# Low parts of streamed weights: a subtraction on VectorE, or an accumulating transfer

## Chip, core and metric

One Trainium2 chip, one core. The metric is the device time of one execution, in microseconds (us). The kernel before takes 723.99 us (median of 3 runs, 723.56 to 726.15).

## What is computed

One layer of an encoder on 512 tokens of width 1024, in float32. In short:

```python
z = rms_norm(x, g_mix) @ W_in                  # 1024 -> latents, rotary key, HGRN2 q, f, i, gate
a = latent_attention(z)                        # 4 heads, softmax over 512 tokens
r = hgrn2(z)                                   # 4 heads, gated recurrence, chunks of 64, two directions
x = x + concat(a, r) @ W_o
h = rms_norm(x, g_ffn)
x = x + (silu(h @ W_gate) * (h @ W_up)) @ W_down          # width 2816
x = x + sigmoid(rms_norm(x, g_ple) @ W_pg) * (p @ W_pp)
```

## The kernel before, in words

**Precision.** TensorE multiplies in float32r, which keeps fewer bits than float32. So each operand is held as two float32r tiles, hi (the value rounded) and lo (the value minus hi), and a product is three matmuls, hi·hi, lo·hi and hi·lo (`mm3`, lines 136 to 139). Features lie on partitions, the 512 tokens on columns.

**Weights.** All large matrices are read from HBM once, in 114 chunks of at most [128, 1024] float32 (512 KB). `weights` (lines 143 to 151) makes one: SP's queue loads it into a tile `raw`, ScalarE rounds it to `whi` (line 130, in `split`), and VectorE subtracts, `wlo = raw - whi` (line 131). `raw` has RAWB = 4 buffers, `whi` and `wlo` WB = 3 each, used in turn. A load waits until both readers of that `raw` buffer are done; a `whi` waits for the matmuls of the chunk three before.

**Stages.** First the latents: five chunks of `w_q`, each with a piece of x, then three of `w_kv` (lines 223 to 257). Then two streams of work are merged (line 921): the latency stream (attention, then the recurrence by head) and the dense stream, which projects with 16 chunks of `w_hf` and 4 of `w_i` and later with the output matrix (`w_oa`, `w_or`) and `w_pp`. The dense stream takes its chunks from `wnext` (lines 560 to 565), which asks for a chunk one ahead of its use (AHEAD = 2) and gives the subtraction of every second chunk of the first 13 to GpSimd, not VectorE (LO_POOL = 14). Last come the feed-forward part (44 chunks of `w_gate` and `w_up`, tiles `ff`; 24 of `w_d`, tiles `dn`) and the embeddings (8 chunks of `w_pg`). One chunk feeds 24 matmuls of 512 columns (21 for most of `w_d`).

**Who else works around it.** In the gates of HGRN2 (lines 606 to 643) ScalarE makes sigmoids and logarithms (lines 613, 631) and has to load a table before each kind; VectorE makes the elementwise steps (lines 616, 618, 627, 628) and GpSimd two products (lines 621, 634). GpSimd also makes the rotary turns (lines 304 to 307), the power -1/2 in every norm (line 164) and the decays (lines 681, 698, 699). VectorE evacuates most PSUM tiles.

**Order.** Each engine runs its instructions in one fixed order and waits on semaphores. The tile framework sets that order when the kernel is built, from a timeline of its own (line 1074), so it is made anew for every version.

Of the kernel before, what the change touches and what calls it, by code (L numbers as in the profile page):

```python
# [8 lines left out]
F32 = mybir.dt.float32  # L9
# [15 lines left out]
# shares of the two streams  # L25
L_TOTAL, D_TOTAL = 97, 135
AHEAD = 2
WB = 3
RAWB = 4
# [3 lines left out]
LO_POOL = 14  # L33
# [3 lines left out]
# columns of the packed per-partition vectors  # L37
V_MIX, V_FFN, V_PLE, V_QA, V_KVA, V_QN, V_KN, V_LB, V_HGO = 0, 8, 16, 24, 26, 28, 29, 30, 46
NV = 50
# columns of the packed rows (the same for every partition)  # L40
R_QN, R_KN = 0, 64
NR = 128
# columns of the constants that depend on shapes alone
# [11 lines left out]
class Slots:  # L55
    """Tiles of one size, handed out by hand: the one that has been free longest comes next."""
# [19 lines left out]
    def part(self, prefix, n):  # L76
        """Slots of their own from the free ones."""
        s = Slots(self.pool, 0, self.prefix)
        s.free.extend(self.free.popleft() for _ in range(n))
        s.count = 1000 * ord(prefix)  # L80
        return s
# [7 lines left out]
def merge(streams):  # L89
    """Runs generators side by side, by the shares of their totals that they have yielded. One that  # L90
    yields a condition waits until it holds."""
    live = [[g, total, 0.0, None] for g, total in streams]
    while live:
        ready = [s for s in live if s[3] is None or s[3]()]
        s = min(ready, key=lambda s: s[2] / s[1])
        s[3] = None
        try:
            y = next(s[0])
        except StopIteration:
            live.remove(s)  # L100
            continue
        if callable(y):
            s[3] = y
        else:
            s[2] += y


def v3(t, a, b=None):
    """A tile's 512 columns as (a, b)."""
    return t.rearrange("p (a b) -> p a b", a=a)  # L110
# [3 lines left out]
def layer_kernel(ctx: ExitStack, tc: tile.TileContext, io, out):  # L114
# [11 lines left out]
    # ---------------------------------------------------------------- helpers  # L126
    def split(hi, lo, src, scale=None, eng=dve):
        """src (times a scale per partition) = hi + lo, each exact in float32r."""
        if scale is None:
            act.activation(hi, src, AF.Copy)  # L130
            eng.tensor_tensor(lo, src, hi, ALU.subtract)  # L131
        else:
            act.activation(hi, src, AF.Copy, scale=scale)
            dve.scalar_tensor_tensor(lo, src, scale, hi, ALU.mult, ALU.subtract)
# [8 lines left out]
    def weights(src, cols, lo_eng=None):  # L143
        """A chunk of weights [128, cols]: its parts hi and lo."""
        nw[0] += 1
        raw = wpool.tile([P, 1024], F32, tag="raw", bufs=RAWB, name=f"raw{nw[0]}")
        hi = wpool.tile([P, 1024], F32R, tag="whi", name=f"whi{nw[0]}")
        lo = wpool.tile([P, 1024], F32R, tag="wlo", name=f"wlo{nw[0]}")
        sp.dma_start(raw[:, :cols], src)
        split(hi[:, :cols], lo[:, :cols], raw[:, :cols], eng=lo_eng or dve)  # L150
        return hi, lo
# [7 lines left out]
    def rsqrt_mean(o, ss, n):  # L159
        """o = (ss / n + eps) ** -0.5, for a few columns."""  # L160
        w = ss.shape[-1]
        v = small.tile([P, 8], F32, tag="rs_v", name="rs_v")
        dve.tensor_scalar(v[:, :w], ss, 1.0 / n, EPS, ALU.mult, ALU.add)  # L163
        pool.tensor_tensor(o, v[:, :w], mhalf[:, :w], ALU.pow)  # L164

    def token_rstd(sq, keep=None):
        """From sums of squares [128 of the features, tokens]: 1/rms by token, tokens on
        partitions [128, 4] and on columns, the same on every partition [128, 512]."""
# [6 lines left out]
        # the diagonal matrices of 1 / rms, summed over the partitions  # L175
# [13 lines left out]
    def squares(acc, src, first):  # L189
        """acc += src ** 2"""  # L190
# [8 lines left out]
    # ---------------------------------------------------------------- inputs  # L199
# [11 lines left out]
    # loads the activation engine's table while the first inputs are under way  # L211
    act.activation(small.tile([P, 1], F32, tag="first", name="first"), mhalf[:, :1], AF.Exp)

    # ---------------------------------------------------------------- input projection, latents
    # the query's latents, features on partitions
    hT = [(A.get(f"hh{k}", F32R), A.get(f"hl{k}", F32R)) for k in range(KT)]
    cq = [B.get(f"cq{m}") for m in range(2)]
    # the tensor engine's clock rises while it is busy
# [4 lines left out]
    for ks in ((0,), (1,), (2, 3), (4, 5), (6, 7)):  # L223
        w = weights(io["w_q"][:, ks[0] * 256 : (ks[-1] + 1) * 256], len(ks) * 256)
# [25 lines left out]
    # those of key and value and the rotary key, tokens on partitions  # L250
    ckv = [B.get(f"ckv{j}") for j in range(NT)]
    for c, ks in enumerate(((0, 1, 2), (3, 4, 5), (6, 7))):
        w = weights(io["w_kv"][:, ks[0] * 320 : (ks[-1] + 1) * 320], len(ks) * 320)
# [20 lines left out]
    # ---------------------------------------------------------------- rotary tables  # L274
# [17 lines left out]
    # cos(r) = sin(pi / 2 - |r|)  # L292
# [9 lines left out]
    def rope(eng, o, x, c, s, t1, t2):  # L302
        """o = x * [cos, cos] + [x2, x1] * [-sin, sin], all [128, a, 64]"""
# [5 lines left out]
    # ---------------------------------------------------------------- lower bounds of the gates  # L309
# [14 lines left out]
    # ================================================================ latent attention  # L324
# [4 lines left out]
    def attention():  # L329
        """Emits the attention in pieces; yields the tensor engine's time for each."""  # L330
        # 1 / rms of the latents, with the one of the input
        sc = cpool.tile([P, 2 * NT], F32, name="sc")  # by token: query, key and value
# [28 lines left out]
        # the shared rotary key, with its gains, turned  # L361
# [8 lines left out]
        def wsmall(name, cols):  # L370
            """A small matrix of two chunks, two halves each."""
# [11 lines left out]
        # keys and values; per head, tokens on partitions: [128, tile, 128]  # L383
# [3 lines left out]
        rt = [A.get(f"rk{j}") for j in range(NT)]  # rotary parts by tile: [128, (key, query) x head, 64]  # L387
# [67 lines left out]
        def features(tok, g):  # L455
            """[128 tokens, tile, 128] to [128 features, tokens], times gains: hi and lo."""
# [9 lines left out]
        def rotary(pr):  # L466
            """Of two heads: the key's parts (hi, hi) and (lo, lo), the query's (hi, lo)."""
# [78 lines left out]
    # ================================================================ HGRN2  # L546
    # 1 at every step but a chunk's first, for the sums along the chunks
# [7 lines left out]
    # chunks of weights for the dense stream, one ahead of its use  # L555
    wlist = deque()
    ahead = deque()
    nd = [0]

    def wnext():  # L560
        while wlist and len(ahead) < AHEAD:
            nd[0] += 1
            on_pool = nd[0] % 2 == 0 and nd[0] < LO_POOL
            ahead.append(weights(*wlist.popleft(), pool if on_pool else dve))
        return ahead.popleft()

    def w_in_tile(d):
        """One tile of 128 of the input projection's columns: [128 columns, tokens]"""
# [11 lines left out]
    def w_in_tokens(evacuate):  # L580
        """512 columns of the input projection, tokens on partitions, 256 at a time."""
# [16 lines left out]
    def gates(heads):  # L598
        """q, and for each direction k and the sums of log f along the chunks."""
# [10 lines left out]
        # one table of the activation engine after the other  # L610
# [13 lines left out]
        for (h, d), f in zs.items():  # L624
            # log f = log max(f, c) + log min(f / c, 1)
# [17 lines left out]
    def together(emit):  # L643
        """The first, whose operand comes last, and the others right behind it."""
        first = emit[0]()
        with tc.issue_after(first.ins):
            for e in emit[1:]:
                e()

    def output_gates():  # L650
        """Features on partitions, with the gains of the output norm."""
# [19 lines left out]
    def decays(h):  # L671
        """Of one head, both directions: queries and keys with the decays that go with them."""
        yield lambda: ("gates", h) in done
        for d in range(2):
# [7 lines left out]
            # exponentials of the sums: to the chunk's middle, from there to its end, to its end  # L682
# [17 lines left out]
            # the same for tiles of two chunks  # L700
# [16 lines left out]
    def within(h):  # L717
        """What reaches a step from its own tile of two chunks, as weights [128 s, tile, 128 t]."""
        pd = BL.get("pd")  # within chunks: [128 (chunk, s), direction, tile, 64 t]
        pd4 = pd.rearrange("p (d j t) -> p d j t", d=2, j=NT)  # L720
        px = BL.get("px")  # from a tile's earlier chunk to its later one
# [27 lines left out]
    def carried(h):  # L749
        """The states before the tiles, both directions."""  # L750
# [50 lines left out]
    def finish(h):  # L801
        """Norm, gate and layout of one head's outputs."""
# [27 lines left out]
    def w_o_half(half, src, banks):  # L830
        """x += (src as rows of features) @ half of the output projection's rows"""
# [92 lines left out]
    def residual(m, o, g, sqacc, hs):  # L924
        """x[m] += o; its squares and its parts hi and lo, with the next norm's gains."""
# [17 lines left out]
    # ---------------------------------------------------------------- feed-forward  # L943
# [41 lines left out]
    # ---------------------------------------------------------------- per-layer embeddings  # L985
    rs3, bc3 = token_rstd(sq3)
    for m in range(KT):
        w = weights(io["w_pg"][m], 1024)
        # the last one in two parts, since nothing is left to overlap with it
# [16 lines left out]
def _layout(inp):  # L1006
# [10 lines left out]
    kp = lambda w: w.reshape(-1, P, w.shape[1])  # [k, 128, columns]  # L1017

    def chunks(w, n):  # n rows of 128 to a chunk: [chunks, 128, n * columns]
# [3 lines left out]
    def tiles(w):  # [tiles of 128 columns, 128, rows / 128 * 128]  # L1023
# [22 lines left out]
    t = tiles(f("w_ple_proj")[0])  # [8, 128, 256]  # L1046
# [32 lines left out]
```

## Time and profile before

| | |
|---|---|
| runs | 723.99 us median, 723.56 to 726.15 |
| span of the profiled execution, first to last instruction | 721.8 us |
| time of the profiled execution as a run | not listed; the median stands 2.2 us over its span |
| TensorE matmul busy | 703.6 us, 97% |
| VectorE, ScalarE, GpSimd busy | 439.3, 309.2, 135.8 us |
| HBM read | 63.68 MB, 91 GB/s over the span |

The profile is of one execution. A busy matmul unit is modelled from pipelined instructions, so it says that work was in flight, not that every cycle was used. "PEclk" is the clock granted to TensorE as a share of its full one. "DMA share" is the busy share of the core's 16 DMA engines. An entry "A <- B" of the waits says that A's engine sat idle until B was done. The chain is the sequence of work that ended last, followed back from the end.

### The profile page before, as it was taken

To read this page: it belongs to the slowest core of one execution; us is meant where nothing else is said; L and a number is where in the kernel's file an instruction comes from. 1 tells how busy PE (TensorE), PEld (TensorE's weight loads), DVE (VectorE), ACT (ScalarE), POOL (GpSimd) and SP (SyncE) were. 2 spreads that over 40 slices of the span, in tenths; PEclk is the share of its full clock that TensorE was granted. 3 is DMA by queue.
4 is the path that set the end of the run, shared out by engine and by line. 5 is a ranking of instruction groups with operands and counts; after the bars stand their busy time and mean duration, and the time that the engine had idled before them with its cause. 6 is when DMAs were issued, how large, how long until landed. Compare 5 with 4: busy or idle time off the path is not lost.

```text
span 721.8 us, 9167 instructions
## 1 busy us (share of the span) xinstructions
PE 703.6 (97%) x3516; PEld 588.5 (82%) x3516; DVE 439.3 (61%) x733; ACT 309.2 (43%) x573; POOL 135.8 (19%) x126
## 2 busy tenths in 40 slices
PE   8999997998999999999999999999999999999997
PEld 6888885897878888788888888888888888888886
DVE  8954469988999984386545334435433444456573
ACT  5566785576554635355233222223222223244341
POOL 7983577010543511001000000000000000000000
PEclk9999999999999999999999999999999999999999
DMA  8432112111034221033232322232233232233211
GB/s 282 167 114 93 59 36 81 59 30 60 15 103 156 60 78 59 30 118 116 96 109 87 104 101 87 91 114 77 79 108 117 90 108 87 78 105 116 89 59 58
DMA packets 22075, 66.36 MB, mean 92 GB/s; under 512 B 2704, under 2 KB 3984, under 8 KB 22032
## 3 DMA queue, kind: packets, MB, share of 16 engines
q1 hardware_dynamic: 22032, 65.79, 28.0%
q8 instruction: 27, 0.44, 0.2%
q14 instruction: 16, 0.13, 0.1%
HBM read 63.68 MB, written 2.10 MB: 91 GB/s over the span
## 4 chain that ended last, share of the span: by engine, by line
PE 85%; DVE 8%; ACT 3%; DMA 2%; issue 1%; SPq 1%; POOL 0%; ACTq 0%; POOLq 0%
PE ff L137 11%; PE ff L138 11%; PE ff L139 11%; PE dn L138 6%; PE dn L137 6%; PE dn L139 6%; PE wi L139 3%; PE wi L137 3%; PE wi L138 3%; PE pg L139 2%; PE pg L138 2%; PE pg L137 2%; PE wo L137 2%; PE wo L139 2%; PE wo L138 2%; PE po L787 1%
## 5 line engine op out<-in xcount | busy, mean ns | idle before, releaser
L130 ACT ACTIVATE whi<-raw 128x1024 fp32r<-128x1024 f32 (+4 forms) x114 | 116.2, 1019 | 286.6 <-issue 103.1
L131 DVE TENSOR_TENSOR wlo<-raw,whi 128x1024 fp32r<-128x1024 f32 (+4 forms) x108 | 133.7, 1240 | 26.1 <-ACT whi L130 24.8
L137 PE MATMUL ff<-hh,whi 128*128 128x512 f32 x352 | 137.0, 390 | 0.1
L138 PE MATMUL ff<-hl,whi 128*128 128x512 f32 x352 | 136.8, 389 | 0.0
L139 PE MATMUL ff<-hh,wlo 128*128 128x512 f32 x352 | 136.8, 389 | 0.0
L957 DVE TENSOR_TENSOR z<-ff,rsbc 128x512 f32<-128x512 f32 x44 | 30.1, 691 | 109.8 <-PE ff L139 109.2
L164 POOL TENSOR_TENSOR rs_tok<-rs_v,mhalf 128x4 f32<-128x4 f32 x3 | 4.7, 1568 | 391.7 <-DVE rs_v L163 391.7
L137 PEld LDWEIGHTS ff<-hh,whi 128*128 128x128 f32 x352 | 66.1, 188 | 14.3 <-ACT whi L130 0.5
L138 PEld LDWEIGHTS ff<-hl,whi 128*128 128x128 f32 x352 | 66.1, 188 | 13.7
L139 PEld LDWEIGHTS ff<-hh,wlo 128*128 128x128 f32 x352 | 66.1, 188 | 13.6
L137 PE MATMUL dn<-ah,whi 128*128 128x512 f32 x176 | 68.5, 389 | 0.0
L138 PE MATMUL dn<-al,whi 128*128 128x512 f32 x176 | 68.5, 389 | 0.0
L139 PE MATMUL dn<-ah,wlo 128*128 128x512 f32 x176 | 68.5, 389 | 0.0
L139 PE MATMUL wi<-hh,wlo 128*128 128x512 f32 x128 | 51.7, 404 | 3.6 <-DVE wlo L131 3.6
L926 DVE TENSOR_TENSOR x<-x,dn 128x512 f32<-128x512 f32 x24 | 16.5, 687 | 60.5 <-PE dn L139 60.5
L138 PE MATMUL wi<-hl,whi 128*128 128x512 f32 x128 | 51.4, 401 | 0.0
L137 PE MATMUL wi<-hh,whi 128*128 128x512 f32 x128 | 51.0, 400 | 0.0
L137 PEld LDWEIGHTS dn<-ah,whi 128*128 128x128 f32 x176 | 33.0, 188 | 6.9
L139 PEld LDWEIGHTS dn<-ah,wlo 128*128 128x128 f32 x176 | 33.0, 188 | 6.8
L138 PEld LDWEIGHTS dn<-al,whi 128*128 128x128 f32 x176 | 33.0, 188 | 6.8
L139 PEld LDWEIGHTS wi<-hh,wlo 128*128 128x128 f32 x128 | 24.5, 191 | 8.9 <-DVE wlo L131 4.0
L138 PEld LDWEIGHTS wi<-hl,whi 128*128 128x128 f32 x128 | 24.4, 191 | 4.9
(287 smaller groups left out, 1361.9 us busy)
## 6 DMA issues: line engine op xcount, KB each, us to landing
raw<-in_w_gate SPq DMA_DIRECT2D x22, 512.0 KB, 3.3
raw<-in_w_up SPq DMA_DIRECT2D x22, 512.0 KB, 3.2
raw<-in_w_hf SPq DMA_DIRECT2D x16, 512.0 KB, 3.7
raw<-in_w_d SPq DMA_DIRECT2D x16, 448.0 KB, 3.2
x<-in_xT SPq DMA_DIRECT2D x16, 256.0 KB, 5.2
raw<-in_w_d SPq DMA_DIRECT2D x8, 512.0 KB, 3.3
raw<-in_w_pg SPq DMA_DIRECT2D x8, 512.0 KB, 3.2
raw<-in_w_i SPq DMA_DIRECT2D x4, 512.0 KB, 3.4
```

The costliest lines, as they stand in the source:

```text
L130: act.activation(hi, src, AF.Copy)
L131: eng.tensor_tensor(lo, src, hi, ALU.subtract)
L137: pe.matmul(o, lhsT=l[0], rhs=r[0], start=start, stop=False)
L138: pe.matmul(o, lhsT=l[0], rhs=r[1], start=False, stop=False)
L139: pe.matmul(o, lhsT=l[1], rhs=r[0], start=False, stop=stop)
L164: pool.tensor_tensor(o, v[:, :w], mhalf[:, :w], ALU.pow)
L787: pe.matmul(po[:, ts(j)], lhsT=l, rhs=r, start=n == 0, stop=n == len(terms) - 1)
L926: dve.tensor_tensor(xT[m], xT[m], o, ALU.add)
L957: dve.tensor_tensor(z, o, bc2, ALU.mult)
```

## The change

For all chunks but the eight early ones (`w_q`, `w_kv`) the subtraction is gone. ScalarE writes the negated, rounded chunk into `wlo` (so `wlo` = -hi), GpSimd's queue issues a DMA that reads the same chunk from HBM a second time and adds it onto `wlo` in SBUF (giving value - hi), and ScalarE writes `whi` from `raw` as before. `raw` now has 3 buffers, `whi` and `wlo` 4 each, and GpSimd makes no subtraction of weights any more.

```diff
-WB = 3
-RAWB = 4
+WB = 4
+RAWB = 3
...
-LO_POOL = 14
...
-    def weights(src, cols, lo_eng=None):
+    def weights(src, cols, early=False):
...
         sp.dma_start(raw[:, :cols], src)
-        split(hi[:, :cols], lo[:, :cols], raw[:, :cols], eng=lo_eng or dve)
+        if early:
+            split(hi[:, :cols], lo[:, :cols], raw[:, :cols])
+        else:
+            act.activation(lo[:, :cols], raw[:, :cols], AF.Copy, scale=-1.0)
+            pool.dma_start(lo[:, :cols], src, accum_op=ALU.add)
+            act.activation(hi[:, :cols], raw[:, :cols], AF.Copy)
         return hi, lo
...
-        w = weights(io["w_q"][:, ks[0] * 256 : (ks[-1] + 1) * 256], len(ks) * 256)
+        w = weights(io["w_q"][:, ks[0] * 256 : (ks[-1] + 1) * 256], len(ks) * 256, early=True)
...
-        w = weights(io["w_kv"][:, ks[0] * 320 : (ks[-1] + 1) * 320], len(ks) * 320)
+        w = weights(io["w_kv"][:, ks[0] * 320 : (ks[-1] + 1) * 320], len(ks) * 320, early=True)
...
-            nd[0] += 1
-            on_pool = nd[0] % 2 == 0 and nd[0] < LO_POOL
-            ahead.append(weights(*wlist.popleft(), pool if on_pool else dve))
+            ahead.append(weights(*wlist.popleft()))
```

## Rows read from the trace of the kernel before

**Rows 1.** The page: busy time by engine; share of the chain by engine.

```profile
PE 703.6 (97%) x3516; PEld 588.5 (82%) x3516; DVE 439.3 (61%) x733; ACT 309.2 (43%) x573; POOL 135.8 (19%) x126
...
PE 85%; DVE 8%; ACT 3%; DMA 2%; issue 1%; SPq 1%; POOL 0%; ACTq 0%; POOLq 0%
```

**Rows 2.** Windows: stretch, length; PE, PEld, DVE, ACT, POOL busy; PEclk, DMA share, GB/s.

```profile
0.00:40.00 40.00, 35.22 (x179) 30.54 (x180) 33.64 (x36) 21.99 (x35) 35.32 (x35) 1.00 0.67 218
...
100.00:220.00 120.00, 111.18 (x643) 93.06 (x642) 110.48 (x236) 76.47 (x140) 45.31 (x32) 0.97 0.17 53
220.00:340.00 120.00, 119.94 (x722) 100.62 (x722) 87.07 (x162) 57.36 (x118) 19.54 (x18) 1.00 0.29 93
340.00:700.00 360.00, 360.00 (x1594) 298.27 (x1593) 169.81 (x212) 108.11 (x132) 1.01 (x1) 1.00 0.29 94
```

**Rows 3.** The chain in order of time: start, us, what.

```profile
4.94 6.54 DMA x<-in_xT
...
97.85 1.28 ACT L613
...
102.70 3.99 DVE z L616 x2
...
113.78 2.22 DVE wlo L131
...
176.41 1.28 ACT L631
...
203.80 1.14 DVE wlo L131
...
209.56 0.22 DVE wlo L131
...
211.95 1.14 DVE wlo L131
```

**Rows 4.** Waits of TensorE over the span: total us, times, longest.

```profile
PE wi L139 <- DVE wlo L131: 3.6, 1, 3.6
```

**Rows 5.** Timeline near 102 us: start, us, engine, line, operation.

```profile
100.86 0.58 DVE L616 TENSOR_SCALAR z<-z,lower,lower 128x512 f32<-128x512 f32 x1 [1.41 <-ACT z L613]
...
102.63 4.07 DVE L616 TENSOR_SCALAR z<-z,lower,lower 128x512 f32<-128x512 f32 x2
...
102.00 1.86 POOL L621 TENSOR_TENSOR z<-z,sig 128x512 f32<-128x512 f32 x1
103.89 2.52 POOL L131 TENSOR_TENSOR wlo<-raw,whi 128x1024 fp32r<-128x1024 f32 x1
```

**Rows 6.** Groups of the page and of the tile raw; ns mean, or min/median/max.

```profile
L130 ACT ACTIVATE whi<-raw 128x1024 fp32r<-128x1024 f32 (+4 forms) x114 | 116.2, 1019 | 286.6 <-issue 103.1
L131 DVE TENSOR_TENSOR wlo<-raw,whi 128x1024 fp32r<-128x1024 f32 (+4 forms) x108 | 133.7, 1240 | 26.1 <-ACT whi L130 24.8
...
L131 POOL TENSOR_TENSOR wlo<-raw,whi x6: 2390/2402/3322, 35.6 to 119.9; 128x1024 fp32r<-128x1024 f32 x6
...
DMA to landing us min/median/max: 3.0/3.3/6.8
```

**Rows 7.** Windows of wlo alone (PE, PEld, DVE, POOL), then of whi on ScalarE alone.

```profile
100.00:220.00 120.00, 41.20 (x120) 23.12 (x120) 12.02 (x9) 5.84 (x2) 0.97 0.17 53
...
340.00:700.00 360.00, 205.25 (x528) 98.95 (x528) 81.01 (x68) 0.00 (x0) 1.00 0.29 94
...
100.00:220.00 120.00, 12.68 (x12) 0.97 0.17 53
...
340.00:700.00 360.00, 70.49 (x68) 1.00 0.29 94
```

**Rows 8.** Timeline at the start: SP's queue, VectorE.

```profile
4.47 0.43 SPq L149 DMA_DIRECT2D raw<-in_w_q  x1
...
5.34 0.42 DVE L131 TENSOR_TENSOR wlo<-raw,whi 128x256 fp32r<-128x256 f32 x1
```

**Rows 9.** Waits of ScalarE over the span: total us, times, longest.

```profile
ACT whi L130 <- PE ff L138: 72.4, 22, 5.8
```

More of the change, by code (lines that the diff above doesn't have):

```diff
@@ L557, in layer_kernel @@
     ahead = deque()
-    nd = [0]
     def wnext():
         while wlist and len(ahead) < AHEAD:
-            nd[0] += 1
-            on_pool = nd[0] % 2 == 0 and nd[0] < LO_POOL
-            ahead.append(weights(*wlist.popleft(), pool if on_pool else dve))
+            ahead.append(weights(*wlist.popleft()))
         return ahead.popleft()
```

## The prediction, made before the changed kernel ran

> **What bounds the kernel now.** I read the page first, then busy time by stretch, the chain, the waits, and the timeline where VectorE was on the chain. The page shows TensorE busy 97% of the span and 85% of the chain, VectorE 8%, ScalarE 3% [rows 1]. A saving on VectorE can only pay where VectorE is on the chain, so the stretch matters more than the 134 us that its subtractions take in all [rows 6].
>
> By stretch there are three cases [rows 2]. From 340 to 700 us TensorE is busy 360.00 of 360 us and VectorE 169.81: no subtraction taken away there can shorten anything. From 220 to 340 us TensorE is busy 119.94 of 120. From 100 to 220 us it is otherwise: VectorE is busy 110.48 of 120 us, TensorE 111.18, its mean clock 0.97. The 8.8 us of idle TensorE in that stretch, and 4.8 us in the first 40, are what can be won. The 4.8 us belong to loads: the chain there sits 6.54 us on a piece of x [rows 3].
>
> The chain between 97 and 216 us says what VectorE was doing when it held the end back. The weights' subtraction is on it four times, 2.22 + 1.14 + 0.22 + 1.14 = 4.72 us [rows 3], and once TensorE itself waits for it, 3.6 us [rows 4], behind the 2.22 us piece. One more piece is hidden under another name. Two instructions of line 616 took 4.07 us together, where one alone takes 0.58 [rows 5]. GpSimd was at line 621 until 103.86 and at a subtraction of weights (2.52 us) until 106.41; VectorE's second instruction ended at 106.70. Read as one waiting out the other, GpSimd's subtraction cost the chain 2.5 us.
>
> **The change, part by part.**
> *Removed from VectorE:* 100 of 108 subtractions. In 100 to 220 us these are 9, 12.02 us [rows 7]; on the chain 4.72 us. *Removed from GpSimd:* 6 subtractions of 2.4 us [rows 6]; on the chain 2.5 us. Together 7.2 us. It cannot be much more: 8.8 us of idle TensorE in that stretch and 3% of 120 us of lost clock (3.6 us) make 12.4 us. What is late next, if the subtractions are gone, is the rest of the gates: VectorE still has 98 of 120 us to do.
>
> *Added to ScalarE:* one negated copy for each of 106 chunks. No row shows it; its nearest is the rounding copy of the same tile, 1.02 us in the mean [rows 6], so 108 us in all. From 340 to 700 us ScalarE goes from 108.11 to 108.11 + 70.49 = 178.6 of 360 [rows 2, 7]: covered by TensorE. From 100 to 220 us, 12 copies, 12.7 us, bring it from 76.47 to 89.2 of 120 [rows 2, 7]. There ScalarE is on the chain where it turns to another function, at 97.85 and 176.41 [rows 3]. Bounds: 0 if every copy falls into an idle moment, 12.7 us if every one lies on the chain; I take two, one per burst, 2.1 us, since ScalarE has a third of that stretch free. The negated copy also stands ahead of `whi`, so `whi` comes 1.0 us later for each chunk; the fourth buffer gives one chunk time more to do it in.
>
> *Added to GpSimd's queue:* 106 DMA issues. The bounds for one are 0.43 us, an issue on SP [rows 8], and 2.4 us, the subtraction that GpSimd now makes [rows 6]; I take the middle, 1.4 us, since neither row is nearer, 148 us in all. GpSimd is almost idle after 340 us (1.01 us busy). Between 100 and 220 us, 12 issues, 17 us against 5.84 us of subtractions taken off, bring it to 57 of 120. In the queue the issue waits for the negated copy; behind it stand the gate products, rotary turns and powers that ScalarE and VectorE wait for. I cost that at nothing in the sum (GpSimd has half the stretch free) and return to it below.
>
> *Added transfers:* 106 second reads of a chunk. Between 340 and 700 us 68 chunks pass, one per 5.29 us, and the plain loads use 29% of the DMA engines [rows 2, 7], so 1.53 us of all sixteen per chunk. Bounds for an accumulating one: as much as a plain load, 1.53 us, and three times that, 4.6 us, if its two reads and its write are each a pass. With the load itself that makes 3.1 to 6.1 us per 5.29. I take two passes, 4.6 us of 5.29: it fits, and costs nothing. The Trainium skill ("Collectives: The Full Stack", Part 3, the bandwidth ceiling) puts a reduce step at two source reads on one ring and half a copy's rate, 32.35 against 62.28 GB/s measured; no run here shows it, and by it the sum would be the same.
>
> Latency between 340 and 700 us is covered too: `whi` waits there for the buffer, not the other way (72.4 us of waits behind the matmuls of line 138 [rows 9]). With four buffer sets the negated copy can start three chunk times, 15.9 us, before its chunk is due; copy 1.0, issue 1.4 and a landing of 3.3 to 6.8 us [rows 6] make 9.2 at most.
>
> *Fewer raw buffers:* at the start the fourth `w_q` load went out at 4.47 us; with three buffers it waits for the first chunk's subtraction, which ends at 5.76 [rows 8], and the x pieces behind it on SP's queue wait too. Bounds 0 and 1.3 us; I take 0.6, since 0 to 40 us is busy with loads (DMA share 0.67 [rows 2]) and those under way fill part of the gap. Later it costs nothing: `raw` is read only by ScalarE then, and is free sooner.
>
> **Sum.** -4.72 - 2.5 + 2.1 + 0.6 = -4.5 us on a span of 721.8. The median of the runs shown lies 2.2 us over that span; the same lies around the new one, so 724.0 - 4.5 = 719.5 us. With ScalarE's bounds and the start's this case reaches from 712 to 724.
>
> **The rivals.**
> *ScalarE takes VectorE's place.* If six or seven of the 12 added copies lie on the chain instead of two, the 7.2 us are given back and the time is 723 to 725. For it: ScalarE's bursts in the gates wait for nobody, and whatever stands in them delays all of them. Against it: 43 of 120 us idle. To it I add that the order of instructions is made anew, and that GpSimd's issues may hold VectorE up as its subtraction did.
>
> *The low parts come late* (slower). A low part is now 1.0 + 1.24 us of work behind its load. It becomes 1.0 + 1.4 + 3.3 to 6.8 us, and the issue first has to come up in GpSimd's queue, which between 97 and 122 us stands full of gate products and turns. That is some 4.5 us later per chunk (3.3 + 2.4 - 1.24). The place is the dense stream up to 340 us, where a chunk is asked for only one ahead. It decides if four of the 12 chunks of 100 to 220 us are needed before they land: 4 x 4.5 = 18 us, against the 4.5 us won: 737.5. That VectorE and GpSimd hold each other up is in the rows already (4.07 us for two instructions [rows 5]). The Trainium skill ("SBUF — State Buffer", SBUF: two separate sides) says that GpSimd cannot write a DMA's descriptors while VectorE is in a two-port mode, which speaks against issuing from GpSimd here; no row shows such an issue.
>
> *The transfers become the bound* (slower). At three passes per accumulating transfer, 6.1 us per chunk against 5.29, every chunk after 340 us adds 0.83 us: 68 x 0.83 = 56 us, 780 us in all. Against it: two passes fit with 0.7 us to spare, which is little.
>
> **How the numbers follow.** 0.5%, 3.6 us, is about what a measurement of this kernel can tell from no change. The forecast, 719.5, has 0.42; ScalarE in VectorE's place 0.26; late low parts 0.20; transfers as the bound 0.12. So faster 0.42, same 0.26, slower 0.32. The range leaves out the last rival and the far ends of the others: 712 to 745. The forecast's own range is 712 to 724.
>
> **What would show it.** Right: TensorE idle in 100 to 220 us falls from 8.8 to about 4 us, no wait of TensorE for `wlo` longer than a microsecond, VectorE under 100 us there, DMA share near 0.87 after 340 us with TensorE still 100% busy. ScalarE in VectorE's place: more ScalarE on the chain between 97 and 180 us. Late low parts: waits of line 139 on a DMA into `wlo`. Transfers: such waits after 340 us, at every chunk. The forecast is wrong if TensorE's idle time grows in any stretch, or if the start costs over 2 us.

## The result and the profile after

The changed kernel takes 727.89 us (median of 18 runs, 725.69 to 731.08) against 723.89 us for the kernel before (18 runs, 723.18 to 726.90). The ratio is 1.0054, 95% interval 1.0041 to 1.0068: 4.0 us slower, where 4.5 us faster was forecast. The profiled execution has a span of 727.1 us and took 728.83 us as a run; before had 721.8 us of span.

The page of the changed kernel: busy time by engine, the queues (packets, MB, share of 16 engines' span), the chain's shares.

```profile
PE 702.0 (97%) x3516; PEld 586.2 (81%) x3516; DVE 325.8 (45%) x633; ACT 402.9 (55%) x679; POOL 203.2 (28%) x226
...
q0 software_dynamic: 15264, 54.53, 42.8%
q1 hardware_dynamic: 22032, 65.79, 29.6%
...
PE 75%; DVE 6%; issue 5%; POOL 5%; ACT 4%; DMA 4%; SPq 0%; ACTq 0%; POOLq 0%
```

The work moved as planned: VectorE went from 439.3 to 325.8 us, ScalarE from 309.2 to 402.9, GpSimd from 135.8 to 203.2 [rows 1]. But the chain now holds DMA at 4% (2% before) and GpSimd at 5% (0%). Queue q0 carries the accumulating transfers. Next the windows (stretch, length; PE, PEld, DVE, ACT, POOL busy; PEclk, DMA share, GB/s).

```profile
0.00:40.00 40.00, 31.81 (x170) 26.97 (x170) 33.20 (x35) 26.02 (x41) 34.51 (x37) 1.00 0.75 229
...
100.00:220.00 120.00, 111.57 (x631) 94.20 (x630) 94.80 (x219) 86.65 (x153) 43.20 (x42) 0.99 0.48 110
220.00:340.00 120.00, 117.26 (x731) 97.32 (x729) 71.18 (x153) 71.39 (x136) 34.54 (x37) 1.00 0.59 140
340.00:700.00 360.00, 359.30 (x1589) 297.69 (x1590) 91.44 (x141) 168.06 (x202) 59.73 (x69) 1.00 0.88 193
```

Against [rows 2]: in 100 to 220 us VectorE lost 15.7 us of work and TensorE's idle time hardly moved, 8.8 to 8.4 us. From 220 to 340 us, where TensorE had been busy 119.94 of 120, it is now idle 2.7 us. The waits of TensorE over the span of the changed kernel (total, times, longest) say for what:

```profile
PE cq L137 <- DVE hl L133: 3.4, 4, 1.6
PE wt L136 <- DVE v L667: 2.9, 2, 1.9
PE av L137 <- DVE mx L518: 2.0, 1, 2.0
...
PE ff L138 <- DMA wlo<-in_w_gate: 1.4, 1, 1.4
PE ff L138 <- DMA wlo<-in_w_up: 1.4, 1, 1.4
...
PE wi L138 <- DMA wlo<-in_w_hf: 1.0, 1, 1.0
```

The wait of 3.6 us for a subtraction [rows 4] is gone. In its place stand three waits for a low part still in transfer, 3.8 us, and between 100 and 220 us new waits for VectorE's other work (`v`, `mx`). The longest entry, 3.4 us for `hl` in the first stage, follows the loads of x at the start; it is taken up with g2 below. The kernel before had three more waits between 100 and 220 us, besides the one of [rows 4]: 2.8, 1.3 and 0.9 us, the longest of them this:

```profile
PE pT L529 <- ACT p L515: 2.8, 1, 2.8
```

The late low parts sit where a stage begins. The chain of the changed kernel (start, us, what), for the first wait, at 39 us:

```profile
30.17 0.95 POOL rnd L288
31.12 9.00 DMA wlo<-in_w_hf
```

GpSimd's queue has a part in this one: the negated copy was done at 29.44 us, and GpSimd, busy with other work of its own, came to the issue at 31.12. Most of GpSimd's 5% of the chain lies ahead of this issue, 22.6 us in the first 40.

The chain at the entry to the feed-forward part:

```profile
310.53 6.91 DMA wlo<-in_w_up
...
329.86 1.03 POOL rs_tok L169
...
330.96 9.69 DMA wlo<-in_w_gate
```

How the wait for `w_up` comes about is seen on ScalarE (timeline: start, us, line, operation):

```profile
305.03 1.04 ACT L153 ACTIVATE wlo<-raw 128x1024 fp32r<-128x1024 f32 x1
305.97 0.70 ACT L132 ACTIVATE hh<-x,vec 128x512 fp32r<-128x512 f32 x1
...
307.11 1.04 ACT L155 ACTIVATE whi<-raw 128x1024 fp32r<-128x1024 f32 x1
...
309.19 1.05 ACT L153 ACTIVATE wlo<-raw 128x1024 fp32r<-128x1024 f32 x1
```

ScalarE is rounding and squaring the residual here, and two copies per chunk are threaded through that. The negated copy of this chunk, the second of the stage, ends at 310.24; only then can its transfer be issued (310.53), and it lands 6.91 us later, with TensorE waiting. The transfer behind the last wait, the fifth of the stage, is issued at 330.96, with two others following within 4 us, and takes 9.69 us. TensorE is ready for these two low parts at 316.7 and 339.3 us, 6.2 and 8.3 us after their issue. For the later one (timeline):

```profile
340.70 0.50 PE L138 MATMUL ff<-hh,wlo 128*128 128x512 f32 x1 [1.40 <-DMA wlo<-in_w_gate]
```

Landing times of the changed kernel, first of the tile `wlo` (accumulating), then of `raw` (plain), us min/median/max:

```profile
DMA to landing us min/median/max: 5.4/7.6/13.6
```

```profile
DMA to landing us min/median/max: 3.1/5.2/10.7
```

The plain loads took 3.0/3.3/6.8 before [rows 6].

### The profile page after: what moved, and what is told of

Same layout as the page of the kernel before. It is cut to its first block, busy times and chain, and to the rows that moved or that the text cites. A ratio compares the mean times of both kernels' runs of the same rounds, so it can differ in the third digit from the quotient of the medians.

```text
span 727.1 us, 9416 instructions
## 1 busy us (share of the span) xinstructions
PE 702.0 (97%) x3516; PEld 586.2 (81%) x3516; DVE 325.8 (45%) x633; ACT 402.9 (55%) x679; POOL 203.2 (28%) x226
## 3 DMA queue, kind: packets, MB, share of 16 engines
q0 software_dynamic: 15264, 54.53, 42.8%
q1 hardware_dynamic: 22032, 65.79, 29.6%
## 4 chain that ended last, share of the span: by engine, by line
PE 75%; DVE 6%; issue 5%; POOL 5%; ACT 4%; DMA 4%; SPq 0%; ACTq 0%; POOLq 0%
PE ff L138 10%; PE ff L136 10%; PE ff L137 10%; PE dn L138 5%; PE dn L137 5%; PE dn L136 5%; PE wi L136 3%; PE wi L138 3%; PE wi L137 3%; PE pg L137 2%; PE pg L138 2%; PE pg L136 2%; DMA wlo<-in_w_gate 1%; DMA wlo<-in_w_hf 1%; POOL sq L249 1%
## 5 line engine op out<-in xcount | busy, mean ns | idle before, releaser
L155 ACT ACTIVATE whi<-raw 128x1024 fp32r<-128x1024 f32 (+1 forms) x106 | 110.7, 1044 | 213.4 <-issue 175.0
L153 ACT ACTIVATE wlo<-raw 128x1024 fp32r<-128x1024 f32 (+1 forms) x106 | 109.3, 1031 | 2.4 <-DMA raw<-in_w_hf 2.1
L136 PEld LDWEIGHTS ff<-hh,whi 128*128 128x128 f32 x352 | 66.1, 188 | 13.6
L154 POOL DMA_DIRECT2D wlo<-in_w_d x24 | 20.7, 862 | 104.0 <-ACT wlo L153 104.0
L154 POOL DMA_DIRECT2D wlo<-in_w_gate x22 | 19.0, 866 | 100.0 <-ACT wlo L153 94.7
L154 POOL DMA_DIRECT2D wlo<-in_w_up x22 | 19.0, 862 | 91.1 <-ACT wlo L153 91.1
```

Source lines behind the costliest of these rows:

```text
L136: pe.matmul(o, lhsT=l[0], rhs=r[0], start=start, stop=False)
L153: act.activation(lo[:, :cols], raw[:, :cols], AF.Copy, scale=-1.0)
L154: pool.dma_start(lo[:, :cols], src, accum_op=ALU.add)
L155: act.activation(hi[:, :cols], raw[:, :cols], AF.Copy)
```

## The experiments

TensorE's instruction list tells which pairs of kernels can be compared directly. Where two lists agree up to some row, the order is held fixed up to there and the difference belongs to the edit; where they differ early, an order made anew is part of the difference. I say for each which it is.

**e1_before_buffers and f1_before_four_sets: the buffers alone.**

```diff
-WB = 3
-RAWB = 4
+WB = 4
+RAWB = 3      # f1: RAWB stays 4
```

> The kernel before with the changed kernel's buffers alone (4 sets of high and low parts, 3 raw buffers), subtraction on VectorE and GpSimd as before. If the buffers cost the start its time: TensorE idle in the first 20 us rises from 4.75 us to about 6.4 us as in the changed kernel, and the time is about 725 us, 1 us over before. If the start's loss has to do with the accumulating transfers: idle stays near 4.75 us and the time is 724 us. If most of the changed kernel's loss comes from buffers: 727 to 728 us.

> The kernel before with 4 sets of high and low parts and its 4 raw buffers, subtraction as before. If the third raw buffer less is what cost the buffers-alone kernel 3.1 us: 723.8 us, as before. If the fourth set, through the order made anew, is the cost: 726 to 727 us.

e1: 726.85 us (724.57 to 729.00), ratio 1.0047, interval 1.0029 to 1.0065. f1: 726.09 us (723.78 to 729.91), 1.0023 (1.0007 to 1.0039). No low part is late in either, and still both are slower than before. TensorE's list differs from that of before early and in some 800 of 3,516 rows, so neither says what a buffer costs. Between each other e1 and f1 differ in a handful of rows: the fourth raw buffer is worth 0.8 us there, within the spread of the runs.

**e2_after_raw4: the changed kernel with four raw buffers.**

```diff
-RAWB = 3
+RAWB = 4
```

> The changed kernel with 4 raw buffers again (and still 4 sets of parts). If 3 raw buffers delay the start: 1 us comes back, 726.9 us, TensorE idle in the first 20 us near 4.8 us; the three stalls of TensorE on low parts (38.8, 316, 339 us) stay at about 4 us together. If raw buffers don't matter: 727.9 us.

727.52 us (725.16 to 731.26), ratio 1.0057 (1.0035 to 1.0080); the same order but for a few rows at the start. The raw buffer is not the loss: 0.4 us. But the three stalls that were to stay did not all stay. Waits of TensorE in this run:

```profile
PE ct L361 <- ACT c L275: 2.7, 1, 2.7
...
PE ff L138 <- DMA wlo<-in_w_gate: 0.4, 1, 0.4
```

At the entry to the feed-forward part the transfers are issued at the same times as in the changed kernel, to within 0.3 us, and the two waits, this one and one for `w_up`, are 0.4 us each, not 1.4. Up to 40 us TensorE waits for ScalarE instead, which was itself held up by a load, and from 40 to 46 us the granted clock is 0.55. So the stalls of one profiled execution do not carry over to another; what the entry costs has to be read from the medians of pairs, below.

**e3_ff_only and e4_dense_only: where the accumulating transfer costs.** Both have 4 sets and 3 raw buffers. e3 accumulates only from the feed-forward part on, e4 only in the dense stream; the rest subtracts as before (e3 with GpSimd's share of it).

```diff
# e4
-                w = weights(io[name][f], 1024)
+                w = weights(io[name][f], 1024, early=True)    # so for w_d and w_pg
# e3
-            ahead.append(weights(*wlist.popleft()))
+            ahead.append(weights(*wlist.popleft(), early=True, lo_eng=pool if on_pool else dve))
```

> The accumulating transfer for the feed-forward and embedding chunks alone; the dense stream's chunks by subtraction on VectorE and GpSimd as before; buffers as in the changed kernel. If low parts that land late at the change of stage are the loss: the stalls at 316 and 339 us stay, 2.8 us, and with 1 us at the start and nothing won between 100 and 220 us the time is 727 to 728 us. If the loss is ScalarE's added copies and the new order in the merged streams: 724 to 725 us.

> The accumulating transfer for the dense stream's chunks alone; feed-forward and embedding chunks by subtraction on VectorE; buffers as in the changed kernel. If late low parts at the change of stage are the loss: the stalls at 316 and 339 us are gone, 725 us. If the loss is ScalarE's added copies and the new order in the merged streams: 727 to 728 us.

e3: 729.71 us (728.73 to 731.39), ratio 1.0087 (1.0073 to 1.0100). e4: 723.83 us (722.15 to 726.56), 1.0002 (0.9991 to 1.0013). Up to the feed-forward part e3 has TensorE's order of e1 and e4 that of the changed kernel. So accumulation from there on, the entry and all that follows, costs 729.71 - 726.85 = 2.9 us in one order and 727.89 - 723.83 = 4.1 us in the other. e3's waits of TensorE name the same place (and 0.9 us for `w_gate`):

```profile
PE ff L138 <- DMA wlo<-in_w_up: 1.7, 1, 1.7
```

**e8_negate_on_vector: ScalarE relieved.**

```diff
-            act.activation(lo[:, :cols], raw[:, :cols], AF.Copy, scale=-1.0)
+            dve.tensor_scalar(lo[:, :cols], raw[:, :cols], -1.0, None, ALU.mult)
```

> The changed kernel with the negated copy made by VectorE and not by ScalarE. If ScalarE's 106 added copies are what takes back the gain in the merged streams: TensorE's idle time from 120 to 180 us falls from 7.8 us to 5 or less and the time is 725 us or less. If late low parts and the buffers are the loss: the stalls at 38, 316 and 339 us stay and the time is 727 to 729 us.

739.76 us (738.35 to 740.88), ratio 1.0212 (1.0198 to 1.0225), in another order. Of its waits of TensorE two matter:

```profile
PE wi L136 <- DVE z L578: 4.9, 2, 4.5
...
PE ff L138 <- DMA wlo<-in_w_gate: 3.3, 1, 3.3
```

The low part is late at the entry with ScalarE relieved, too, and VectorE becomes the one waited for. This speaks against ScalarE's copies as the cause of the late low part. What they cost elsewhere it does not settle, since the order is new.

**e5_dense_old_buffers, e6_dense_late, e7_ramp: without the fourth set.** All have WB = 3 and RAWB = 4. e5 is e4 otherwise; e6 also subtracts for the first four dense chunks; e7 is e6 with accumulation in the feed-forward part after its first eight chunks.

```diff
-WB = 4
-RAWB = 3
+WB = 3
+RAWB = 4
# e6, e7
+            ahead.append(weights(*wlist.popleft(), early=nw[0] < 12))
```

> The accumulating transfer for the dense stream's chunks alone, now with the buffers of before (3 sets, 4 raw). Buffers alone cost the kernel before 3.1 us, and the dense stream's transfers won 3.0 us against that. If the two add up: 723.8 - 3.1 = 720.7 us, TensorE idle in the first 20 us near 4.8. If the fourth set is what lets the dense transfers hide: 724 us or more, with longer waits of TensorE on low parts before 340 us.

> As the run before, but the first four chunks of the dense stream by subtraction on VectorE too, so that GpSimd's queue has no transfer to issue while it works on the first norm. If the low part that lands late near 38 us (1.1 to 1.7 us of stall) and the issues in GpSimd's queue ahead of the norm's power are a cost of the change: that wait is gone and the time is 1 to 2 us under the run before, 719 to 720 us. If they are covered: no difference.

> As the run before, with the accumulating transfer also for the feed-forward and embedding chunks, except the first eight. If the loss there is only the low parts that land late at the entry (stalls at 316 and 339 us) and the steady stretch is free: the same time as the run before within 1 us, DMA share 0.85 or more and TensorE idle under 1 us from 360 to 700 us. If the transfers are nearly the bound or ScalarE's copies cost in the steady stretch: 3 us or more over the run before.

e5: 744.45 us (739.91 to 746.75), ratio 1.0275 (1.0246 to 1.0304). e6: 744.16 us, 1.0282 (1.0265 to 1.0298). e7: 752.50 us, 1.0407 (1.0388 to 1.0426). e5 is 20.6 us slower than e4. TensorE's order is not quite the same: by their traces the two differ in some 230 of 3,516 rows, the first at 16 us, so this is the price of the buffers together with what the order made of them. e5's waits of TensorE:

```profile
PE wi L136 <- DVE z L578: 8.9, 1, 8.9
PE wo L138 <- DMA wlo<-in_w_or: 5.0, 2, 3.6
PE wi L138 <- DMA wlo<-in_w_hf: 3.6, 1, 3.6
```

Two of them are low parts come late. The longest one goes back to VectorE and GpSimd at 107 to 122 us; of e5's timeline, GpSimd's and then VectorE's:

```profile
106.87 3.88 POOL L154 DMA_DIRECT2D wlo<-in_w_hf  x1 [0.58 <-ACT qt L448]
```

```profile
109.87 0.41 DVE L620 TENSOR_SCALAR k<-z 128x512 f32<-128x512 f32 x1
110.21 0.41 DVE L629 TENSOR_SCALAR t<-z 128x512 f32<-128x512 f32 x1
...
115.47 6.19 DVE L640 TENSOR_TENSOR_SCAN t<-mF,z 128x512 f32<-128x512 f32 x1
```

An issue that takes 0.86 us elsewhere took 3.88 us while VectorE ran these short operations back to back, and the gate product behind it in GpSimd's order came that much later. The scan, 6.19 us where the next one takes 1.21, runs beside GpSimd's products; why it takes so long is not shown. e6 subtracts at first and has the same wait of 8.9 us, so a late low part at the start of the dense stream is not behind it. e7 shows what the fourth set does later. Its wait of TensorE, and the window from 340 to 700 us:

```profile
PE dn L138 <- DMA wlo<-in_w_d: 5.8, 4, 2.6
```

```profile
340.00:700.00 360.00, 354.24 (x1557) 292.00 (x1556) 92.56 (x138) 159.00 (x189) 55.50 (x63) 1.00 0.81 181
```

TensorE is busy 354.24 of 360 us, against 359.30 in the changed kernel and 360.00 in f3 below, which also has four raw buffers and subtracts at the entry: the fourth set is what hides the landing in the steady stretch.

**f2_dense_only_44 and f3_hybrid_44: versions meant to win.** Both with four sets and four raw buffers; f2 is e4 otherwise, f3 subtracts for the first two dense and the first eight feed-forward chunks and accumulates for the rest.

```diff
-RAWB = 3
+RAWB = 4
# f3
+            ahead.append(weights(*wlist.popleft(), early=nw[0] < 10))
...
+                w = weights(io[name][f], 1024, early=f < 4)
```

> The accumulating transfer for the dense stream's chunks alone, 4 sets and 4 raw buffers. If the dense stream's transfers win 3 us and the third raw buffer less costs 3 us, both apart from each other: 720 to 721 us, faster than both kernels. If the two don't add up, since each version has its own order: 723 to 728 us.

> The changed kernel with 4 sets and 4 raw buffers, and subtraction for the first two chunks of the dense stream and the first eight of the feed-forward part: accumulating transfers everywhere but at the entries to a stage. If the late low parts at the entries are the loss of the feed-forward part and the steady stretch is free: within 1 us of the run before, no wait of TensorE for a low part over 0.5 us after 300 us. If the fullness of the DMA engines costs by itself: 2 us or more over the run before.

f2: 725.27 us (721.02 to 729.80), ratio 1.0015 (0.9991 to 1.0039). f3: 728.88 us (727.40 to 729.71), 1.0056 (1.0038 to 1.0074). f3 is 3.6 us over f2, which by its expectation would point to the fullness of the DMA engines. Its trace does not: nothing waits for a low part after 300 us, TensorE is busy 360.00 of 360 us from 340 us on, and the time was lost between 100 and 220 us (TensorE busy 108.88 of 120, 113.41 in f2), in an order that differs from 43 us on. At 113 us, in the dense stream, it waits 2.4 us for a low part.

**f4_half_more: half as many bytes again, onto a spare tile that nothing reads.**

```diff
+            pool.dma_start(spare[nw[0] % 2], src[:, :512], accum_op=ALU.add)
```

> The changed kernel with one more accumulating transfer per chunk, of 512 columns, onto a spare tile that nothing reads: accumulated bytes up by half, with everything else as it was. By the time of packets in the changed kernel (0.88 of the DMA engines from 340 to 700 us, two thirds of it accumulating) the engines would be asked for 1.17 of their time: each chunk takes about 6.2 us and not 5.3, some 60 us more after 340 us, with waits of TensorE on low parts at every chunk. If the packets' time overstates what the engines have to give: under 10 us more.

843.44 us in a single run. It does not answer its question: the order of GpSimd put all 106 extra transfers between 2.2 and 347.6 us, none into the steady stretch. What the transfers could still bear there is therefore not measured. It shows something else. GpSimd waits in its own queue for a spare tile's previous transfer to land (116.7 us in all), and what stands behind the issue waits too: VectorE sits 14.4 us idle for one gate product of GpSimd before it can make `v`, for which TensorE waits. GpSimd's longest group of waits, then TensorE's:

```profile
POOL spare L159 <- DMA spare<-in_w_d: 34.2, 16, 4.2
```

```profile
PE wt L136 <- DVE v L671: 29.9, 3, 17.6
```

**g1_ff_entry_subtracted: the entry alone.** The changed kernel, with the subtraction on VectorE for the first eight chunks of the feed-forward part.

```diff
-                w = weights(io[name][f], 1024)
+                w = weights(io[name][f], 1024, early=f < 4)
```

> Only the first eight chunks of the feed-forward part get their low part by subtraction again; everything else is the changed kernel, dense stream included, so the order up to 300 us should stay near the changed kernel's. Theory (low parts late at the entry to the feed-forward part): no wait of TensorE for a low part at 316 or 339 us, about 3 us of TensorE time back, 724 to 725. Rival (the loss is the order made anew and the buffers, and those waits are made good elsewhere): 727 to 728 as the changed kernel.

725.01 us (723.54 to 728.84), ratio 1.0017 (1.0005 to 1.0029): 2.9 us less than the changed kernel. TensorE's lists agree in their first 1,698 of 3,516 rows, up to the feed-forward part. No wait for `w_gate` or `w_up` is left, and the last two windows are these:

```profile
220.00:340.00 120.00, 118.72 (x740) 99.21 (x739) 81.42 (x162) 66.30 (x130) 29.45 (x30) 1.00 0.47 121
340.00:700.00 360.00, 360.00 (x1594) 298.26 (x1593) 93.68 (x144) 168.88 (x202) 59.76 (x69) 1.00 0.86 189
```

TensorE gained 1.5 and 0.7 us in them, 2.2 of the 2.9. Its accumulating transfers start again at 344.4 us, and from 340 us on TensorE is busy throughout at a DMA share of 0.86.

**g2_before_other_share, g3_after_other_share, g4_ff_entry_other_share: another order.** The kernel before, the changed kernel and g1, each with the share by which the dense stream is merged at 136, not 135. Nothing else is computed or moved.

```diff
-L_TOTAL, D_TOTAL = 97, 135
+L_TOTAL, D_TOTAL = 97, 136
```

> The kernel before with one number of the merge changed, 135 to 136, so that nothing is computed or moved otherwise but the order of the two streams is made anew. Theory (an order made anew costs or gives some microseconds by itself): 722 to 728, at a distance from 723.9 of the size of the change's own effect. Rival (the order is robust, and differences of 2 to 4 us belong to the edits): 723.5 to 724.5.

> The changed kernel with the same one number changed, 135 to 136. Theory (late low parts at the entries cost 3 to 4 us in any order): 726 to 730, again with waits for a low part near the entry to the feed-forward part. Rival (the loss hangs on this one order): the time falls to 724 or below, or the waits for a low part are gone.

> g1's edit (first eight chunks of the feed-forward part by subtraction) on top of g3's order (share 136), whose trace shows TensorE waiting 2.1 us twice for a low part at 322 and 350 us. Theory (the entry to the feed-forward part costs 3 to 4 us in any order): 733.5 to 735 against g3's 737.9, both waits gone, and up to there the same as g3. Rival (it holds for one order only, or the waits are made good elsewhere): 737 to 738.

| share | before | changed | changed, entry by subtraction |
|---|---|---|---|
| 135 | 723.89 | 727.89, 1.0054 (1.0041 to 1.0068) | 725.01, 1.0017 (1.0005 to 1.0029) |
| 136 | 735.27, 1.0157 (1.0143 to 1.0170) | 737.89, 1.0172 (1.0146 to 1.0198) | 729.76, 1.0085 (1.0063 to 1.0107) |

All ratios are to the kernel before at 135. I had expected up to 4 us from a new order; it was 11.4 us. Between two profiles a part of such a difference is not the order's: the lists of TensorE, ScalarE and VectorE in g2 and in the kernel before are the same up to 150 us, and yet TensorE is busy 32.83 of the first 40 us in g2 and 35.22 in the kernel before [rows 2]. So executions of the same instructions differ there by 2.4 us, with the loads:

```profile
0.00:40.00 40.00, 32.83 (x177) 28.43 (x178) 33.71 (x36) 21.95 (x35) 34.87 (x35) 1.00 0.66 216
```

And the entry, taken out of g3 with TensorE's order the same up to it, gave 8.1 us, twice what was expected. In g3 TensorE waited there twice, 2.1 us each:

```profile
PE ff L138 <- DMA wlo<-in_w_gate: 4.2, 2, 2.1
```

That is half of the 8.1. The windows around the two waits, of g3,

```profile
320.00:330.00 10.00, 7.88 (x27) 5.80 (x27) 8.33 (x14) 9.08 (x14) 1.72 (x2) 0.83 1.03 261
...
345.00:360.00 15.00, 12.97 (x50) 10.20 (x49) 5.67 (x9) 8.78 (x11) 2.24 (x3) 0.89 0.95 234
```

and of g4,

```profile
320.00:330.00 10.00, 10.00 (x45) 8.28 (x45) 8.58 (x12) 2.58 (x5) 0.00 (x0) 1.00 0.33 107
...
345.00:360.00 15.00, 15.00 (x68) 12.41 (x67) 8.35 (x13) 11.36 (x15) 2.62 (x3) 1.00 0.66 144
```

show the other half. In g3 the granted clock is 0.83 and 0.89 there, which means that part of the time went at the lower of its two levels (1.2 instead of 2.4 GHz), where g4 has 1.00 throughout. TensorE makes 18 matmuls fewer in each window; at g4's pace of 0.22 us each, 36 of them are 7.9 us, against 8.1 between the medians. So close an agreement is luck: g3's runs spread from 732.79 to 739.92 us, and the two profiled executions stand 10.7 us apart. The waits of 1.4 us in the changed kernel have no such aftermath: its clock is 1.00 from 220 us to 700 us, in the windows above. But g3's wait of 1.5 us at 39 us, for the dense stream's first low part, has one (g4 waits 0.7 us there, and its clock is 1.00):

```profile
40.00:45.00 5.00, 4.66 (x15) 3.71 (x16) 2.42 (x11) 2.60 (x16) 3.67 (x7) 0.66 1.05 270
```

Waits with a fallen clock behind them are also the larger part of g2's 11.4 us. A window of the kernel before,

```profile
160.00:180.00 20.00, 17.22 (x104) 14.89 (x102) 17.03 (x42) 13.14 (x23) 1.06 (x1) 0.91 0.17 54
```

and of g2, which waits twice for the softmax's low part there, 4.0 us at the longest (from 180 to 200 us its clock is 0.78, against 1.00):

```profile
160.00:180.00 20.00, 12.82 (x43) 8.87 (x42) 13.31 (x34) 10.80 (x17) 1.26 (x1) 0.71 0.00 0
```

**g5_entry_share_134 and g6_entry_share_130: g1 in two more orders.** The edit of g1, with the share at 134 and at 130.

> g1 (first eight chunks of the feed-forward part by subtraction) with the merge's share 134. Theory (once the entry is mended the rest of the change is worth -5.5 to +1.1 us against before, by the order it lands in): 718 to 735 by the order, with no wait of TensorE for a low part of w_gate or w_up. Rival (the accumulating transfer costs a fixed few us elsewhere): a wait for a low part somewhere after 300 us again. Faster than 723.9 would be a version that beats both.

> The same with the share 130: another order. Theory: 718 to 735, no wait for a low part of w_gate or w_up, the time set by TensorE's idle time between 100 and 220 us. Rival: a wait for a low part after 300 us again.

g5: 722.79 us (720.78 to 725.73), ratio 0.9979 (0.9965 to 0.9993). g6: 737.54 us (734.78 to 739.77), 1.0179 (1.0158 to 1.0200). Neither waits for a low part of `w_gate` or `w_up`. g5 is the fastest version here, 1.1 us under before: its interval lies below 1, by less than the 0.5% that the prediction set as the mark. g6's loss is between 100 and 220 us:

```profile
100.00:220.00 120.00, 103.54 (x559) 88.09 (x558) 98.27 (x218) 81.28 (x145) 40.61 (x39) 0.93 0.41 88
```

## Why the prediction was wrong

Forecast and measurement are 8.4 us apart, 719.5 against 727.89. By g1 2.9 us of this are one step, a latency put at nothing. The larger part, 5.5 us, is another: a gain that did not come.

**The step that failed: latency costed at nothing.** "Latency between 340 and 700 us is covered too" is true of the steady stretch, and it was worked out for that alone. The entry to the feed-forward part entered the sum at no cost. There no chunk has three chunk times of lead: the copies stand among the residual's work on ScalarE, and several transfers start together and land in 6.9 and 9.7 us, with 6.2 and 8.3 us to spare. A subtraction takes 1.24 us once `whi` is there [rows 6]. The entry alone cost 2.9 us by g1, and 8.1 in the order of g3, where the clock fell behind the waits as well; with all that follows it, it was 2.9 by e3 against e1, 4.1 by e4 and 2.3 by e2 against f2 (f2's runs spread over 9 us). In single executions the waits vary, as e2 shows. The rival of late low parts named the mechanism and what to look for (waits of that line of `mm3` on a DMA into `wlo`); it had the place and the size wrong. It put them in 100 to 220 us, four chunks of 4.5 us; they came one per place, at 39, 317 and 339 us. In other versions they came where it put them, too: 2.4 us at 113 us in f3, and with three sets 3.6 to 4.1 us between 130 and 220 (e5 to e7).

**The second failed step: -7.2 us read off the chain.** The subtractions did leave the chain, and VectorE's 94.80 us between 100 and 220 are under the 100 forecast. But TensorE's idle time there stayed at 8.4 us, where about 4 was forecast, and the page's waits only changed names; what was won there is in the clock, 0.97 before and 0.99 after. Pieces of a chain are not savings: when one goes, the chain can run through another engine. Between 97 and 220 us VectorE's part of it fell from 54.2 to 30.6 us; ScalarE's rose from 15.2 to 24.1, GpSimd's from 1.2 to 8.0 (gate products and rotary turns, in the queue that the sum has at nothing) and TensorE's from 45.9 to 55.8. Which part of that the change brought and which the order, no run separates. For the order of all engines was made anew, and by g2 that alone can move the time by as much as 11.4 us. So the size of the gain without the entry is not settled: g1 stands 1.1 us above before, g4 5.5 us below g2, and the four orders of g1's edit spread from 722.79 to 737.54 us. The forecast of -4.5 lies between the two differences at an equal share, but none of the four reached 719.5. What is shown is that the gain was not got in this order, and that the entry took 2.9 us of the 4.0.

Two of the prediction's own signs of being wrong came. TensorE's idle time grew from 220 to 340 us, by 2.7 us, at the entry. And TensorE is busy 3.4 us less in the first 40, where a start of over 2 us was the mark: 1.0 of that is the late low part at 39 us, and the rest is no more than executions of the same instructions differ by there (2.4 us, g2).

**ScalarE: the copies were sized about right, the rival is not excluded.** Two added copies on the chain were taken, 2.1 us. Between 97 and 240 us two are on it, 1.45 us, and a rounding copy, which the kernel before makes too:

```profile
109.78 0.95 ACT whi L155
110.73 0.68 ACT wlo L153
...
129.23 0.77 ACT wlo L153
```

ScalarE is busy 86.65 us from 100 to 220, 89.2 by the forecast. So it did not take back 7.2 us by six or seven copies on the chain. But the sign that the prediction named for this rival, more ScalarE on the chain between 97 and 180 us, did come: 24.1 us against 13.6. It is softmax and gate work, with five table loads on the chain where three were (at 101.78, 153.25, 161.36, 171.46 and 111.69 us, the last right behind the two copies above):

```profile
111.69 1.28 ACT L633
```

In g3, with the same copies in another order, it is 14.1 us, and in e8, without them on ScalarE, 10.9. So the copies in ScalarE's bursts may be part of why the gain did not come; no run holds the order fixed to show it.

**Right: the transfers were not the bound.** From 340 us TensorE is busy 359.30 of 360 us, the DMA share 0.88 (0.87 forecast), and g1 is busy for all 360. By the packets' time an accumulated byte costs (42.8 / 54.53) / (29.6 / 65.79) = 1.74 times a plain one, where two passes were taken. The Trainium skill ("Collectives: The Full Stack", Part 3) gives a reduce step half of a copy's rate; this trace shows somewhat less than that penalty, for another kind of transfer.

**Sized wrong, without effect.** The issue on GpSimd took 0.86 us, not 1.4. Landing was 5.4 to 13.6 us, not 3.3 to 6.8: the bounds were rows of plain loads with nothing beside them. The steady stretch bore it, since three chunk times are 15.9 us. The raw buffer at the start was put at 0.6 us; the pairs whose TensorE order agrees but for a few rows give +0.8 (e1 against f1), +0.4 (the changed kernel against e2) and -1.4 (e4 against f2), so nothing that can be told from zero. The range of "this case", 712 to 724, does not follow from the bounds named for it either: with ScalarE's 12.7 us and the start's 1.3 the sum reaches to some 731.

**Open.** What the dense stream's accumulation is worth by itself. Three pairs have the same buffers and differ in it, e4 against e1, f2 against f1 and the changed kernel against e3: -3.0, -0.8 and -1.8 us, each less than the 4.5 forecast, and each with another order. And how much more the transfers could bear after 340 us, since f4 put none there.

## What to carry to other kernels

When an operation of 1 us on an engine becomes a transfer of 5 to 14 us, work out the lead that it has where a stage begins, not only in the steady stretch, and leave the short way in place for the first chunks of each stage. When the order of instructions is made anew with every edit, measure first what a neutral edit does to the time: here 11.4 us, nearly three times the effect under study. Then compare only kernels whose order agrees up to the edit, as g1 with the changed kernel, and by many runs, since the stalls of one execution need not be those of the next.

## What the runs showed of the hardware

**A wait can cost twice its length.** Two waits of 2.1 us in g3 cost 7.9 us of matmuls, since the granted clock fell to 0.83 and 0.89 around them. The length of the wait alone does not tell: waits of 1.4 us in the changed kernel left it at 1.00, one of 1.5 us in g3 was followed by 0.66 over 5 us, and one of 1.6 us at the same place in g5 left it at 1.00.

**Plain loads beside accumulating transfers land later.** With the 106 accumulating transfers the plain loads' median landing went from 3.3 to 5.2 us; in e4, where no accumulating transfer runs beside the later chunks' loads, it is 3.3 again over the span, with a longest of 9.3. From 350 to 690 us it is 5.8 in the changed kernel and 3.2 in e4. Whether the addition does it, the second read or GpSimd's queue, no run separates; the same holds for the accumulating transfers' own 7.6 us.

```profile
DMA to landing us min/median/max: 3.0/3.3/9.3
```

**An issue on GpSimd can take four times as long.** 3.88 us in e5 against 0.86, while VectorE ran operations of 0.41 us without a gap. The Trainium skill ("SBUF — State Buffer", SBUF: two separate sides) says that GpSimd can't write a DMA's descriptors while VectorE is in a two-port mode. The row fits that; no run took VectorE's operations away to show it. In the changed kernel the longest issue near the gates was 0.96 us (1.60 over the span, at 33.72 us), so the prediction's fear of it did not come about there.

**Negating a [128, 1024] chunk** took VectorE 0.68 us (median in e8, longest 2.74) and ScalarE 1.04 us.
